# Two edits to a two-layer mixer kernel: weight halves summed by an accumulating transfer, and a gate product in 512-column matmuls

## The chip, the cores and the metric

The kernel runs on one core of one Trainium2 chip. The metric is the device time of one execution in microseconds (us); less is better. The time before is the median of three runs.

## The reference

Two layers act on 256 tokens of width 2048, together with 256 context tokens, all in float32. Layer 0 is a Fourier mixer, layer 1 an attention mixer. The parts that the change touches are the input projection of layer 0 and the gate of layer 1:

```python
def _fourier_branch(h, w_in, w_mix):
    b, n, _ = h.shape
    u, z = jnp.split(h @ w_in, 2, axis=-1)
    ug = u.reshape(b, n, FNET_GROUPS, FNET_GROUP_DIM).astype(jnp.float32)
    f = jnp.fft.fft2(ug, axes=(1, 3), norm='ortho').real.astype(h.dtype)
    f = jnp.einsum('bngc,gcd->bngd', f, w_mix).reshape(b, n, D_BRANCH)
    return f * jax.nn.silu(z)

def _attention_branch(h, hc, w_in, sink, rows, cols, need_ctx):
    ...
    q, k, v, z = jnp.split(h @ w_in, [D_BRANCH, D_BRANCH + kvw, D_BRANCH + 2 * kvw], axis=-1)
    ...                      # banded attention with a sink, 64 heads of 64, 8 key/value heads
    y = jnp.moveaxis(o, 0, 1).reshape(b, n, D_BRANCH) * jax.nn.silu(z)
```

Each layer computes shift, scale and gate from `silu(c) @ ada_w + ada_b`, normalizes its input, runs its branch and adds `gate * (y @ w_out)`. A last normalization follows. There are 16 Fourier groups of 256 channels, and the branch is 4096 wide.

## The kernel before

Every large product is made of three matmuls (`mm3`, L72): each operand is split into a high part (a cast to fp32r on ScalarE, L60) and a low part (the rest, formed on VectorE, L61), and high*high, high*low and low*high are accumulated in PSUM.

The program is written with a tile framework. It gives each engine a queue that runs in order, and a scheduler with a simulated timeline decides the order of the instructions in these queues. So the order on an engine is fixed when the program is built, and an instruction that waits holds up all that stand behind it.

**Projection of layer 0 (`load_uh`, `split_uh`, and the loop over `g`).** The two-dimensional transform is real and symmetric, so channel `j` and channel `256-j` of a group are used as a sum and a difference. The weights are laid out so that one load of 1016 KB (`raw`, a pool of three buffers, issued on SyncE's queue) holds for 8 blocks of 128 rows two halves of 127 channels side by side: `v[:, :, 0, :]` and `v[:, :, 1, :]`. A group has two such loads (`kh` 0 and 1). For each, `load_uh` forms the difference in a tile `wm` (GpSimd, L122) and the sum in place in `raw` (VectorE, L123). `split_uh` then makes four tiles from them (`wml`, `wmh`, `wpl`, `wph`) in a pool of eight, so one group fills the pool, and a half can be split only when TensorE has used the same half of the group before. On TensorE a group runs: `load_m(g)` (10 matmuls, on the mixing weights, `mt` formed by VectorE in L239 and L240), the differences' part (48 matmuls), the mix of the group before (14), the sums' part (48). The results of the mix go to DRAM by two transfers on GpSimd's queue (`fd`, L386).

**The rest of layer 0.** The gate `z` and the output product run after this, with the sums for the adaptive norms on VectorE beside them.

**Layer 1 (`emit_unit`, and the loop that calls it).** The attention loop has 66 steps. A step forms the scores of one half-unit (`stage_s`), the products with the values of an earlier one (`stage_o`), the transposes of the one before (`stage_t`), and two "filler" units between them: an eighth of a query projection, half of a gate block, or a step of the output product. A gate block `("z", b)` is 128 channels of `z`: 16 blocks `k` of the inner dimension, three matmuls of 256 columns each, into the first half of a PSUM bank. `hx1[k]` holds the high part of the input in columns 0 to 255 and the low part in columns 256 to 511. After the last `k`, ScalarE takes tanh (L782) and VectorE completes silu (L783). There are 32 gate blocks.

Of the kernel before, what the change touches and what calls it, by code (L numbers as in the profile page):

```python
# [10 lines left out]
F32 = mybir.dt.float32  # L11
F32R = mybir.dt.float32r
AF = mybir.ActivationFunctionType
ALU = mybir.AluOpType
AX = mybir.AxisListType

P = 128
D = 2048
KT = D // P
DB = 4096  # L20
NB = DB // P
N = 256
# [6 lines left out]
def tile_dit(ctx: ExitStack, tc: tile.TileContext, a: dict, out: bass.AP):  # L29
    nc = tc.nc  # L30
    V, S, PE, GP = nc.vector, nc.scalar, nc.tensor, nc.gpsimd
# [8 lines left out]
    def psum():  # L40
        return pp.tile([P, 512], F32, tag="ps", name="ps")
# [30 lines left out]
    def mm3(o, wh, wl, xh, xl, start, stop):  # L72
        PE.matmul(o, wh, xh, start=start, stop=False)  # L73
        PE.matmul(o, wh, xl, start=False, stop=False)  # L74
        PE.matmul(o, wl, xh, start=False, stop=stop)  # L75
# [43 lines left out]
    def load_uh(g, kh, ld=raw):  # L119
        v = ld(a["wu"][g, kh])[:, : 8 * 2 * 127].rearrange("p (k s c) -> p k s c", k=8, s=2)  # L120
        m = wsp.tile([P, 8, 127], F32, tag="ws", name="wm")
        GP.tensor_tensor(m, v[:, :, 0, :], v[:, :, 1, :], op=ALU.subtract)  # L122
        V.tensor_tensor(v[:, :, 0, :], v[:, :, 0, :], v[:, :, 1, :], op=ALU.add)  # L123
        return v[:, :, 0, :], m

    def split_uh(v, m):
# [8 lines left out]
    def load_u(g):  # L135
        return [split_uh(*f) for f in [load_uh(g, kh) for kh in range(2)]]
# [10 lines left out]
    with tc.tile_pool(name="st", reuse_waits="tile", bufs=1, side="right") as st:  # L147
# [55 lines left out]
        for nb in range(4):  # L203
# [11 lines left out]
            for j in range(4):  # L215
                o = psum()
                for s in range(2):
                    for tt in range(2):
                        q = slice(j * P, (j + 1) * P)
# [90 lines left out]
    for g in range(G):  # L310
        if g == 1:
            w = []
            for kh in range(2):
                f = load_uh(g, kh)
                with tc.issue_after(f0_end):
                    w.append(split_uh(*f))
        else:
            w = load_u(g) if g else w0
# [30 lines left out]
        if g == 0:  # L349
            o = psum()  # L350
            ov = o[0:32, 0:260].rearrange("p (s j) -> p s j", s=2)
            for k in range(KT):
                h, l = hx[k]
                q = slice(k * 32, (k + 1) * 32)
# [75 lines left out]
    with tc.tile_pool(name="yp", reuse_waits="tile", bufs=32) as ypool:  # L430
# [19 lines left out]
        with tc.tile_pool(name="zp", reuse_waits="tile", bufs=2) as zp:  # L450
# [10 lines left out]
            for kg in range(4):  # L461
# [7 lines left out]
                for j in range(4):  # L469
                    k = kg * 4 + j  # L470
                    wh, wl = w[j // 2]
                    for b in range(4):
                        q = slice((j % 2) * 512 + b * P, (j % 2) * 512 + (b + 1) * P)
# [6 lines left out]
            for b in range(4, NB):  # L480
# [3 lines left out]
                o = psum()  # L484
                for k in range(KT):
                    wh, wl = w[k // 8]
                    q = slice((k % 8) * P, (k % 8 + 1) * P)
# [29 lines left out]
        for i in range(32):  # L517
            sw, kg = i // 16, i % 16
            if kg == 0:
                o = [psum() for _ in range(8)]  # L520
# [11 lines left out]
            for j, b in [(j, b) for b in range(8) for j in range(2)] if edge else [(j, b) for j in range(2) for b in range(8)]:  # L532
                q = slice(b * P, (b + 1) * P)
# [16 lines left out]
    o = psum()  # L550
# [8 lines left out]
    o = psum()  # L559
# [27 lines left out]
    with tc.tile_pool(name="h1", reuse_waits="tile", bufs=16) as h1p:  # L587
        hx1 = []
        v2 = [[None] * 2 for _ in range(4)]
        kT = []  # L590
        with tc.tile_pool(name="kvp", reuse_waits="tile", bufs=2) as kvp:
            hc1 = []
            for k in range(KT):
# [3 lines left out]
                for s, h in ((0, hx), (1, hc)):  # L597
                    q = slice(s * N, (s + 1) * N)
# [5 lines left out]
            o = [[psum() for _ in range(2)] for _ in range(4)]  # L604
            for kg in range(8):
                w = ws_split(raw(a["wkv"][kg]))
                for j in range(2):
                    k = kg * 2 + j
                    wh, wl = w[j]
                    for tb in range(4):  # L610
                        h = (hx1, hc1)[tb // 2][k]
                        c = (tb % 2) * P
                        for kv in range(2):
                            q = slice(kv * 512, (kv + 1) * 512)
# [15 lines left out]
            for hp in range(4):  # L630
                o = psum()
# [10 lines left out]
        with tc.tile_pool(name="at", reuse_waits="tile", bufs=2) as at:  # L642
# [19 lines left out]
            def o1_step(k, os_, wh, wl):  # L662
                while len(yh) <= min(k + 2, NB - 1) and (len(yh) < 20 or fin):
                    y_split(len(yh))
                for tb in range(2):
                    mm3(os_[tb], yh[k][:, tb * P : (tb + 1) * P], yh[k][:, N + tb * P : N + (tb + 1) * P], wh, wl, k == 0, k == NB - 1)
# [13 lines left out]
            def finish_q(hk, oq):  # L680
                qr = []
                for tb in range(2):
                    t = act()
                    if hk == 0:
                        roped(t, oq[tb], tb, actp, "act")
                    else:
                        t0 = act()
                        S.copy(t0, oq[tb])
                        roped(t, t0, tb, actp, "act", GP)
                    qr.append(t)  # L690
                prep_kk(hk)
                for p2 in range(2):
                    defer.append((slot[0], lambda p2=p2: q_turn(hk, p2, qr)))
# [38 lines left out]
            def prep(u):  # L732
                kind, n, i, _ = u
                if kind == "o":
                    if i == 1:
                        return None
                    return w1_next()
                src = (kind, n, i // 2)
                if src not in raws1:
                    raws1[src] = raw(a["wq"][n, i // 2] if kind == "q" else a["wz1"][n])  # L740
                return half_split(raws1[src], i % 2)
# [3 lines left out]
            def emit_unit():  # L745
                if pos[0] >= len(ulist):
                    return
                u = ulist[pos[0]]
                if pos[0] not in ready:
                    ready[pos[0]] = prep(u)  # L750
                if pos[0] + 1 < len(ulist):
                    ready[pos[0] + 1] = prep(ulist[pos[0] + 1])
                w = ready.pop(pos[0])
                pos[0] += 1
                kind, n, i, o = u
                if kind == "o":
                    if n == 0 and i == 0:
                        oA.extend([psum(), psum()])
                    if i == 0:
                        curw[0] = w  # L760
                    o1_step(n * 2 + i, oA, *(t[:, i * 512 : (i + 1) * 512] for t in curw[0]))
                    return
                wh, wl = w
                if kind == "q":
                    if i == 0:
                        o += [psum(), psum()]
                    for j in range(2):
                        k = i * 2 + j
                        q = slice(j * 512, (j + 1) * 512)
                        for tb in range(2):  # L770
                            mm3(o[tb], hx1[k][:, tb * P : (tb + 1) * P], hx1[k][:, N + tb * P : N + (tb + 1) * P], wh[:, q], wl[:, q], k == 0, k == KT - 1)
                    if i == 7:
                        finish_q(n, o)
                else:
                    if i == 0:
                        o.append(psum())
                    for k in range(i * 8, i * 8 + 8):
                        q = slice((k % 8) * P, (k % 8 + 1) * P)
                        mm3(o[0][:, 0:N], wh[:, q], wl[:, q], hx1[k][:, 0:N], hx1[k][:, N : 2 * N], k == 0, k == KT - 1)
                    if i == 1:  # L780
                        th = at.tile([P, N], F32, tag="th", name="th", bufs=3)
                        S.activation(th, o[0][:, 0:N], AF.Tanh, scale=0.5)  # L782
                        V.scalar_tensor_tensor(th, th, 1.0, o[0][:, 0:N], op0=ALU.add, op1=ALU.mult)  # L783
                        szs[n] = th
                        emit_y(n)

# [2 lines left out]
            def emit_y(blk):  # L789
                if blk not in szs or (blk, 1) not in obs or blk in ydone:  # L790
                    return
                ydone.add(blk)
                if blk % 2 == 0:
                    y1.append(act())
                V.scalar_tensor_tensor(y1[blk // 2][:, (blk % 2) * N : (blk % 2 + 1) * N], obs[blk, 1], 0.5, szs.pop(blk), op0=ALU.mult, op1=ALU.mult)
# [61 lines left out]
            for i in range(first):  # L857
                emit_unit()
                if i >= 8 and defer:
                    defer.pop(0)[1]()  # L860

            def filler():
                j = slot[0]
                slot[0] += 1
                emit_unit()
                if defer and defer[0][0] + 2 < j:
                    defer.pop(0)[1]()
# [16 lines left out]
        with tc.tile_pool(name="fin", reuse_waits="tile", bufs=1) as fp:  # L884
# [28 lines left out]
            o = [[psum() for _ in range(2)] for _ in range(2)]  # L913
            for kg in range(16):
                w = ws_split(raw(a["wo1b"][kg]))
                for j in range(2):
                    k = kg * 2 + j
                    wh, wl = w[j]
                    for tb in range(2):
                        for c in range(2):  # L920
                            q = slice(c * 512, (c + 1) * 512)
# [4 lines left out]
            o = [psum() for _ in range(2)]  # L926
# [148 lines left out]
```

## Time and profile before

| | us |
|---|---|
| median of three runs | 1885.29 (1885.03 to 1887.53) |
| the profiled execution | 1881.67 |
| its span | 1879.8 |

| engine | busy us | share of the span | instructions |
|---|---|---|---|
| TensorE, matmuls (PE) | 1835.5 | 98% | 10433 |
| TensorE, weight loads (PEld) | 1583.7 | 84% | 10433 |
| VectorE (DVE) | 1396.9 | 74% | 2711 |
| ScalarE (ACT) | 929.7 | 49% | 1602 |
| GpSimd (POOL) | 240.5 | 13% | 206 |

The mean granted clock of TensorE is 0.988. The projection of layer 0 lies between about 100 and 348 us, the attention loop of layer 1 between about 1180 and 1700 us.

How to read the rows: a row of a group of instructions has line, engine, operation, output <- inputs, shapes, count | busy us, mean ns of one | idle time of the engine before them and what ended it. A row of a timeline begins with the start in us from the start of the span and the duration in us. Matmuls overlap, so the duration of one is longer than the distance to the next. A row of waits says which engine waited at which line for what: total us, times, longest us. A row of a DMA queue has packets, MB, and the share of the 16 DMA engines' time; a row of transfers has their count, KB each, and the median us from issue to landing.

### The profile page before, as it was taken

To read this page: it belongs to the slowest core of one execution; us is meant where nothing else is said; L and a number is where in the kernel's file an instruction comes from. 1 tells how busy PE (TensorE), PEld (TensorE's weight loads), DVE (VectorE), ACT (ScalarE), POOL (GpSimd) and SP (SyncE) were. 2 spreads that over 40 slices of the span, in tenths; PEclk is the share of its full clock that TensorE was granted. 3 is DMA by queue.
4 is the path that set the end of the run, shared out by engine and by line. 5 is a ranking of instruction groups with operands and counts; after the bars stand their busy time and mean duration, and the time that the engine had idled before them with its cause. 6 is when DMAs were issued, how large, how long until landed. Compare 5 with 4: busy or idle time off the path is not lost.

```text
span 1879.8 us, 27439 instructions
## 1 busy us (share of the span) xinstructions
PE 1835.5 (98%) x10433; PEld 1583.7 (84%) x10433; DVE 1396.9 (74%) x2711; ACT 929.7 (49%) x1602; POOL 240.5 (13%) x206
## 2 busy tenths in 40 slices
PE   6899999999999999999999999999999999999997
PEld 4479999888888888888888787889989989998886
DVE  4469999787777789687984835788778787787455
ACT  3334444442222233324221524888888888887343
POOL 0034444200000000000000001112221220200001
PEclk8899999999999999999999999999999999999999
DMA  9965555656665546763575323333333333434543
GB/s 365 387 258 201 200 202 189 233 218 232 244 232 214 224 179 256 269 236 134 224 270 222 129 90 135 135 132 115 129 118 135 113 135 126 167 132 169 192 179 135
DMA packets 60533, 359.67 MB, mean 191 GB/s; under 512 B 7601, under 2 KB 7745, under 8 KB 25329
## 3 DMA queue, kind: packets, MB, share of 16 engines
q1 hardware_dynamic: 49104, 324.83, 46.7%
q0 software_dynamic: 6720, 25.34, 3.6%
q10 hardware_dynamic: 4576, 7.74, 1.3%
q8 instruction: 82, 1.34, 0.3%
q14 instruction: 51, 0.41, 0.1%
HBM read 345.30 MB, written 12.59 MB: 190 GB/s over the span
## 4 chain that ended last, share of the span: by engine, by line
PE 88%; DVE 4%; DMA 3%; issue 2%; ACT 1%; POOL 1%; ACTq 0%; POOLq 0%; DVEq 0%; SPq 0%
PE ps L73 25%; PE ps L74 25%; PE ps L75 25%; PE ps L830 3%; PE ps L845 2%; PE ps L844 2%; PE ps L811 1%; PE ps L810 1%; DMA raw<-in_awp 1%; DMA raw<-in_wu 1%; PE ps L180 1%; POOL wm L122 1%; DVE mt L239 1%; DVE wpl L61 1%; DVE wml L61 0%
## 5 line engine op out<-in xcount | busy, mean ns | idle before, releaser
L61 DVE TENSOR_TENSOR wl<-raw,wh 128x1024 fp32r<-128x1024 f32 x333 | 423.7, 1274 | 291.1 <-ACT wh L60 288.8
L60 ACT CAST wh<-raw 128x1024 fp32r<-128x1024 f32 x333 | 349.4, 1051 | 566.2 <-PE ps L74 507.0
L74 PE MATMUL ps<-act,wh 128*128 128x512 f32 x1024 | 398.3, 389 | 0.0
L73 PE MATMUL ps<-act,wh 128*128 128x512 f32 x1024 | 394.1, 389 | 0.0
L75 PE MATMUL ps<-act,wl 128*128 128x512 f32 x1024 | 391.1, 389 | 0.0
L73 PEld LDWEIGHTS ps<-act,wh 128*128 128x128 f32 x1024 | 192.2, 188 | 39.8
L75 PEld LDWEIGHTS ps<-act,wl 128*128 128x128 f32 x1024 | 192.2, 188 | 39.9
L74 PEld LDWEIGHTS ps<-act,wh 128*128 128x128 f32 x1024 | 192.2, 188 | 39.8
L417 DVE CUSTOM_DVE_ANT_0 raw<-raw,cb 128x512 f32<-128x512 f32 x256 | 172.5, 688 | 16.4 <-DMA raw<-in_adw 12.6
L73 PE MATMUL ps<-h,wh 128*128 128x256 f32 x512 | 147.1, 287 | 0.0
L74 PE MATMUL ps<-h,wh 128*128 128x256 f32 x512 | 144.8, 283 | 0.0
L75 PE MATMUL ps<-h,wl 128*128 128x256 f32 x512 | 144.7, 283 | 0.0
L417 DVE CUSTOM_DVE_ANT_0 junk<-raw,cb 128x512 f32<-128x512 f32 x192 | 131.7, 686 | 14.1 <-ACT cb L409 7.1
L74 PE MATMUL ps<-wl,h 128*128 128x512 f32 x320 | 125.5, 392 | 1.4 <-DVE wl L61 1.4
L73 PE MATMUL ps<-wh,h 128*128 128x512 f32 x320 | 124.7, 398 | 0.2 <-ACT h L600 0.2
L75 PE MATMUL ps<-wh,h 128*128 128x512 f32 x320 | 124.9, 392 | 0.0
L122 POOL TENSOR_TENSOR wm<-raw 128x1016 f32<-128x1016 f32 x32 | 87.7, 2740 | 195.8 <-DMA raw<-in_wu 195.3
L812 DVE CUSTOM_DVE_ANT_0 ps<-ps,mask,nsink 128x512 f32<-128x512 f32 x128 | 92.0, 753 | 10.9 <-PE ps L811 10.6
L73 PEld LDWEIGHTS ps<-h,wh 128*128 128x128 f32 x512 | 97.3, 190 | 1.3
L815 ACT ACTIVATE p<-ps,mx 128x512 f32<-128x512 f32 x128 | 87.3, 687 | 21.3 <-DVE mx L812 20.3
L74 PEld LDWEIGHTS ps<-h,wh 128*128 128x128 f32 x512 | 97.4, 190 | 0.0
L75 PEld LDWEIGHTS ps<-h,wl 128*128 128x128 f32 x512 | 97.3, 190 | 0.0
(302 smaller groups left out, 3785.3 us busy)
## 6 DMA issues: line engine op xcount, KB each, us to landing
raw<-in_wz SPq DMA_DIRECT2D x64, 1024.0 KB, 4.8
raw<-in_adw SPq DMA_DIRECT2D x64, 1024.0 KB, 4.8
raw<-in_awp SPq DMA_DIRECT2D x32, 1024.0 KB, 9.5
raw<-in_wo SPq DMA_DIRECT2D x32, 1024.0 KB, 5.5
raw<-in_wq SPq DMA_DIRECT2D x32, 1024.0 KB, 4.8
raw<-in_wu SPq DMA_DIRECT2D x32, 1016.0 KB, 5.4
raw<-in_wo1b SPq DMA_DIRECT2D x16, 1024.0 KB, 4.8
act<-in_xT POOLq DMA_DIRECT2D x32, 256.0 KB, 5.2
```

The costliest lines, as they stand in the source:

```text
L60: S.copy(h, src)
L61: V.tensor_tensor(l, src, h.bitcast(F32), op=ALU.subtract)
L73: PE.matmul(o, wh, xh, start=start, stop=False)
L74: PE.matmul(o, wh, xl, start=False, stop=False)
L75: PE.matmul(o, wl, xh, start=False, stop=stop)
L122: GP.tensor_tensor(m, v[:, :, 0, :], v[:, :, 1, :], op=ALU.subtract)
L417: V.tensor_tensor_reduce(junk if s == 0 and i < 3 else wf, wf, cb[:, s, kq * 512 : kq * 512 + 512], 1.0, 0.0, ALU.mult, ALU.add, acc[:, i, ...
L812: V.tensor_tensor_reduce(o, o, mask[:, tb, :], -0.125, nsink[:, i : i + 1], ALU.add, ALU.min, mx[:, tb : tb + 1])
L815: S.activation(pt[:, tb, :], so[tb], AF.Exp, bias=mx[:, tb : tb + 1], scale=-1.0, accum_out=sm[:, tb : tb + 1])
L830: PE.transpose(o[:, (kt * 2 + tb) * P : (kt * 2 + tb + 1) * P], pt[:, tb, c : c + P], ident)
L844: PE.matmul(oo[:, 0:N], st, ph[:, q], start=kb == 0, stop=False)
L845: PE.matmul(oo[:, 0:N], st, pl[:, q], start=False, stop=kb == 3)
```

## The change

In the projection, the first two groups stay as they were. For groups 2 to 15 the difference is formed on VectorE, and the sum by a transfer from GpSimd's queue that reads the second half once more from HBM and adds it to the first half in `raw`. It may go out only when VectorE has read the first half.

In layer 1 the gate product multiplies `wh` with high and low part at once (512 columns: high product in columns 0 to 255, cross product in 256 to 511) and `wl` with the high part (256 columns, added to the first half). The two halves of the bank are added at the end: ScalarE copies the second half to a tile `zs` (one buffer), VectorE adds the first, and tanh and the completion of silu read `zs`.

```diff
     def load_uh(g, kh, ld=raw):
         v = ld(a["wu"][g, kh])[:, : 8 * 2 * 127].rearrange("p (k s c) -> p k s c", k=8, s=2)
         m = wsp.tile([P, 8, 127], F32, tag="ws", name="wm")
-        GP.tensor_tensor(m, v[:, :, 0, :], v[:, :, 1, :], op=ALU.subtract)
-        V.tensor_tensor(v[:, :, 0, :], v[:, :, 0, :], v[:, :, 1, :], op=ALU.add)
+        if g < 2:
+            GP.tensor_tensor(m, v[:, :, 0, :], v[:, :, 1, :], op=ALU.subtract)
+            V.tensor_tensor(v[:, :, 0, :], v[:, :, 0, :], v[:, :, 1, :], op=ALU.add)
+        else:
+            V.tensor_tensor(m, v[:, :, 0, :], v[:, :, 1, :], op=ALU.subtract)
+            b = a["wu"][g, kh].rearrange("p (k s c) -> p k s c", k=8, s=2)[:, :, 1, :]
+            nc.gpsimd.dma_start(out=v[:, :, 0, :], in_=b, accum_op=ALU.add)
         return v[:, :, 0, :], m
...
                     for k in range(i * 8, i * 8 + 8):
                         q = slice((k % 8) * P, (k % 8 + 1) * P)
-                        mm3(o[0][:, 0:N], wh[:, q], wl[:, q], hx1[k][:, 0:N], hx1[k][:, N : 2 * N], k == 0, k == KT - 1)
+                        for part in (0, 1) if k < KT - 1 else (1, 0):
+                            if part == 0:
+                                PE.matmul(o[0], wh[:, q], hx1[k], start=k == 0, stop=k == KT - 1)
+                            else:
+                                PE.matmul(o[0][:, 0:N], wl[:, q], hx1[k][:, 0:N], start=False, stop=False)
                     if i == 1:
                         th = at.tile([P, N], F32, tag="th", name="th", bufs=3)
-                        S.activation(th, o[0][:, 0:N], AF.Tanh, scale=0.5)
-                        V.scalar_tensor_tensor(th, th, 1.0, o[0][:, 0:N], op0=ALU.add, op1=ALU.mult)
+                        zs = at.tile([P, N], F32, tag="zs", name="zs", bufs=1)
+                        S.copy(zs, o[0][:, N : 2 * N])
+                        V.tensor_tensor(zs, o[0][:, 0:N], zs, op=ALU.add)
+                        S.activation(th, zs, AF.Tanh, scale=0.5)
+                        V.scalar_tensor_tensor(th, th, 1.0, zs, op0=ALU.add, op1=ALU.mult)
```

## The prediction

> **What bounds the kernel now.** I read the page first: the busy shares and the chain that ended last.
>
> ```profile
> span 1879.8 us, 27439 instructions
> ...
> PE 1835.5 (98%) x10433; PEld 1583.7 (84%) x10433; DVE 1396.9 (74%) x2711; ACT 929.7 (49%) x1602; POOL 240.5 (13%) x206
> ...
> PE 88%; DVE 4%; DMA 3%; issue 2%; ACT 1%; POOL 1%; ACTq 0%; POOLq 0%; DVEq 0%; SPq 0%
> ```
>
> TensorE is the bound over the whole run, so an edit pays only where it takes time off TensorE, or removes one of its few gaps; it costs where it opens a gap. Next come the two stretches that the change touches: the middle of the Fourier projection (150 to 350 us) and the attention loop of layer 1 (1200 to 1700 us). Columns: stretch, length, busy time of each engine, granted clock, share of the DMA engines, GB/s.
>
> ```profile
> 150.00:350.00 200.00, 198.26 (x1629) 197.10 (x1628) 184.97 (x241) 91.74 (x181) 87.69 (x64) 1.00 0.61 211
> 1200.00:1700.00 500.00, 500.00 (x3427) 463.08 (x3427) 398.12 (x762) 419.31 (x815) 86.89 (x73) 1.00 0.36 129
> 250.00:300.00 50.00, 50.00 (x417) 50.00 (x416) 48.92 (x56) 22.96 (x44) 22.18 (x13) 1.00 0.57 197
> ```
>
> In the projection TensorE lacks 1.74 us in 200, VectorE is 92% busy, and the DMA engines are busy 57% of the time where the stage runs evenly (250 to 300). In layer 1 TensorE has no gap, and ScalarE is 84% busy. Nearly all of the 1.74 us lies in three places, read from stretches of 2 us:
>
> ```profile
> 178.00:180.00 2.00, 1.57 (x13) 1.36 (x12) 2.00 (x4) 2.00 (x4) 0.00 (x0) 1.00 0.45 147
> 208.00:210.00 2.00, 1.37 (x11) 1.16 (x11) 2.00 (x4) 2.00 (x4) 0.00 (x0) 1.00 0.49 117
> 346.00:348.00 2.00, 1.47 (x12) 1.25 (x11) 1.76 (x6) 1.44 (x4) 1.10 (x3) 1.00 1.01 381
> ```
>
> In the first two VectorE is full (2.00): 0.43 + 0.63 = 1.06 us lost to a late VectorE. The third is the hand-over to the next stage, which the change leaves alone.
>
> The timeline of TensorE gives the rhythm of one group of the projection: the sums' part (wph), load_m (ch), the differences' part (wmh), the mix (pqh), the next sums.
>
> ```profile
> 282.99 0.29 PE L73 MATMUL ps<-act,wph 128*127 128x260 f32 x1
> ...
> 288.90 0.28 PE L73 MATMUL ps<-mh,ch 128*128 128x256 f32 x1
> ...
> 290.08 0.28 PE L73 MATMUL ps<-act,wmh 128*127 128x256 f32 x1
> ...
> 295.80 0.28 PE L73 MATMUL ps<-mh,pqh 127*128 127x256 f32 x1
> ...
> 297.47 0.29 PE L73 MATMUL ps<-act,wph 128*127 128x260 f32 x1
> ```
>
> A group takes 297.47 - 282.99 = 14.48 us, and two weight halves must be loaded, combined and split in it.
>
> **Layer 1: the gate product.** Before, each of 16 k takes three 256-column matmuls; after, one of 512 columns (wh against high and low side by side) and one of 256. What a matmul costs is the distance between starts, not its duration, since they overlap:
>
> ```profile
> 1281.28 0.28 PE L74 MATMUL ps<-h,wh 128*128 128x256 f32 x1
> ...
> 1283.92 0.28 PE L75 MATMUL ps<-h,wl 128*128 128x256 f32 x1
> ```
> ```profile
> 1259.79 0.39 PE L73 MATMUL ps<-wh,h 128*128 128x512 f32 x1
> ...
> 1261.60 0.39 PE L75 MATMUL ps<-wh,h 128*128 128x512 f32 x1
> ```
> ```profile
> 1253.76 0.40 PE L73 MATMUL ps<-wh,h 128*128 128x512 f32 x1
> 1254.00 0.40 PE L74 MATMUL ps<-wl,h 128*128 128x512 f32 x1
> 1254.23 0.28 PE L845 MATMUL ps<-pl,act 128*128 128x256 f32 x1
> 1254.35 0.28 PE L844 MATMUL ps<-ph,act 128*128 128x256 f32 x1
> ```
>
> The first pair spans 22 starts of the gate product: 2.64 / 22 = 0.120 us each, 0.360 per k. The second spans 8 starts of 512 columns: 1.81 / 8 = 0.226. So a k would take 0.226 + 0.120 = 0.346. Where both widths stand mixed (third fence) a 512 takes 0.23 to 0.24 and the 256 behind it 0.12, so 0.35 or 0.36. The saving per k is 0.014 us by the clean rows, 0.010 by the mixed 0.35, nothing by 0.36; times 16 k and 32 blocks, 512 in all: 7.2, 5.1 or 0. I take 6 us: the new sequence alternates, as the mixed rows do, but regularly, so I set it between the first two.
>
> Each of the 32 blocks gains a ScalarE copy and a VectorE add, both 128x256 out of PSUM; tanh and the following multiply now read SBUF. The nearest rows are the two operations there today:
>
> ```profile
> L783 DVE SCALAR_TENSOR_TENSOR th<-th,ps 128x256 f32<-128x256 f32 x32 | 13.2, 412 | 0.0
> L782 ACT ACTIVATE th<-ps 128x256 f32<-128x256 f32 x32 | 12.1, 379 | 0.0
> ```
>
> So 32 x 0.38 = 12 us more on ScalarE: (419 + 12) / 494 = 87% instead of 84%; 32 x 0.41 = 13 us on VectorE: (398 + 13) / 494 = 83%. Neither is the bound, and softmax results are used one loop step after they are made, so I cost this at 0. The cover is that step's slack; if it is gone, what is queued behind the copy on ScalarE are the exponentials and the weight casts, and TensorE waits for both. In the queues as built the tanh does not stand right behind its copy: exponentials and a weight cast lie between, which cover the wait for VectorE's add. The bank is given back after the add, as it was after the multiply. The bound is all of the saving (6 us).
>
> **Projection: VectorE and GpSimd.** For 14 of 16 groups (28 halves) VectorE drops the add and takes the subtraction of the same shape; GpSimd drops the subtraction and issues a transfer.
>
> ```profile
> L122 POOL TENSOR_TENSOR wm<-raw 128x1016 f32<-128x1016 f32 x24 | 66.4, 2768 | 92.6 <-DMA raw<-in_wu 92.6
> L61 DVE TENSOR_TENSOR wpl<-raw,wph 128x1016 fp32r<-128x1016 f32 x26 | 40.2, 1545 | 0.0
> L123 DVE TENSOR_TENSOR raw<-raw 128x1016 f32<-128x1016 f32 x25 | 30.3, 1211 | 8.8 <-POOL wm L122 8.8
> L386 POOL DMA_DIRECT2D fd<-ft x28 | 15.4, 551 | 14.6 <-ACT ft L385 14.1
> L239 DVE TENSOR_TENSOR mt<-m 128x256 f32<-128x256 f32 x12 | 13.7, 1144 | 0.0
> L240 DVE TENSOR_TENSOR mt<-m 128x256 f32<-128x256 f32 x12 | 5.0, 416 | 0.0
> ```
>
> VectorE's own count is even: 1.21 us out, 1.21 in. But L239 and L240 do the same work and take 1144 and 416 ns: L239 runs beside GpSimd's subtraction and waits for it. With that gone VectorE gets back 12 x 0.73 = 9 us from L239 and 26 x (1.545 - 1.211) = 9 us from wpl, and the 1.06 us of gaps go. The Trainium skill, page "SBUF — State Buffer", section "Who interferes with whom", says that a VectorE instruction with two SBUF inputs contends with a GpSimd instruction that reads SBUF; the trace agrees with the two rows above. I book -1 us (bounds 0 and -1.7). What is late next is TensorE itself, which is full.
>
> The new wait on VectorE: the subtraction now waits for the raw load itself, where GpSimd waited before (92.6 us in the row). In the changed program's order the subtraction of half 0 stands just before the evacuation of an earlier group's sums. The raw load is issued when an older buffer's split is done:
>
> ```profile
> SPq L46 <- DVE wpl L61: 172.4, 26, 9.4
> ```
> ```profile
> q0 software_dynamic: 3020, 9.91, 12.9%
> ...
> raw<-in_wu SPq DMA_DIRECT2D x23, 1016.0 KB, 5.4
> fd<-ft POOLq DMA_DIRECT2D x28, 256.0 KB, 3.8
> ...
> act<-in_xT POOLq DMA_DIRECT2D x12, 256.0 KB, 5.4
> ```
>
> The load lands 5.4 us after its issue; three buffers at two per 14.48 us give 21.7 us per turn, so it is there in time. Cost 0, unless loads become late (below).
>
> **The accumulating transfer.** No row shows one. It reads 508 KB again from HBM, reads as much of the destination, and writes it, in runs of 508 bytes. Two questions.
>
> Latency: in the built order, the transfer of half 0 of group g+1 goes out as the sums' part of g-1 ends (288.90 in the rows), and the cast that needs it stands behind the mix, in the sums' part of g; its target buffers come free halfway through that part, at 297.47 + 2.95 = 300.4. That is 12 us without any wait, and some 16 before the casts and splits queued behind it on ScalarE and VectorE make the next differences' part late. A 256 KB transfer of GpSimd lands in 3.8 to 5.4 us. For 508 KB, worst case: 5.4, plus 5.4 for the bytes (next paragraph), plus an issue eight times as long as the 0.55 us row, for eight times as many runs (4.4): 15 us. At best 6. So latency is covered, and GpSimd's queue too: two issues of at most 4.4 and two stores of 0.55 in 14.48 us. The stores queued behind an issue are late by up to 4.4 us, in a group of slack.
>
> Throughput: GpSimd's queue moved 9.91 MB in 12.9% of 200 us, so 2.6 us of all 16 engines per MB, 1.35 us for 0.52 MB. A second read of the same size makes 2.7; short pieces at half that rate make 5.4. Per group the engines have 0.57 x 14.48 = 8.25 us of work now. Two transfers make that 10.95, 13.65 or 19.05 us, against 14.48. I take the middle, since the read of the destination is certain and nothing here shows short pieces to be slow: 94% full, hidden under TensorE, cost 0.
>
> The Trainium skill, page "DMA: Bandwidth & Descriptors", section "Specifications", speaks against this: 512 B is the smallest transfer at line rate, and below it the engine reads, modifies and writes. The runs here have 508. No run here shows it; by that rule the upper case would hold.
>
> **The sum.** -6 (gate) -1 (gaps) = -7 us. From the profiled execution, 1881.7 us (its span 1879.8 and 1.9 around it), that gives 1874.7; the median of the three timed runs stands 3.6 higher, at 1885.3, which gives 1878.
>
> **The rivals.**
> *The DMA engines become the bound* (slower). Place: groups 2 to 15, from the point where one transfer takes more than (14.48 - 8.25) / 2 = 3.1 us of all engines, 2.3 times the plain rate. Then the raw loads come late, the subtraction waits in VectorE's queue with everything behind it, and TensorE starves. Halfway between the two upper cases, 4.05 us each: 16.35 us a group, +1.87 x 14 = +26, less 6 from the gate: 1905. At 5.4 each: 4.57 x 14 = +64, 1943. For it: 94% is near full already, and the runs are short. Against: 2.7 us is below the point. This is the skill's rule with a price.
> *The gate's saving does not come* (no change). Either the 512 takes 0.24 in the alternation, or ScalarE at 87% makes TensorE wait in a loop that had no gap: 0 to 3 us of the 6 left, 1881 to 1884. For it: the mixed rows. Against: the clean rows, and idle time on ScalarE of 16%.
> That the change would not do what it says is excluded: the changed program as built has the 28 transfers on GpSimd's queue and the 512-column matmuls on TensorE's.
>
> **How the numbers follow.** Forecast 0.55, DMA-bound 0.32, saving lost 0.13. The forecast's own range is 1875 (gate 7.2, gaps 1.7, and a little) to 1881. The range reaches from 1874 to 1910, which takes in the DMA rival up to 4.2 us a transfer and leaves out its tail, about 0.15. 0.2%, about what a measurement of this kernel can tell from no change, is 3.8 us: faster 0.55, same 0.13, slower 0.32.
>
> **What would show it.** Right: groups of the projection still 14.5 us apart, DMA share there near 0.9, L239's successor near 0.42 us, no "POOL wm" rows after group 1; in layer 1, 0.346 to 0.35 us per k and no idle row on TensorE. Wrong: a period above 15 us with ScalarE's wph cast waiting for DMA, a landing over 16 us, or an issue on GpSimd of many microseconds; in layer 1, gaps before the transposes of p.

## The result, and the profile after

| | before | after | ratio, 95% interval |
|---|---|---|---|
| median of 20 runs each, us | 1886.82 | 1892.33 | 1.0023 (1.0012 to 1.0034) |
| the same on another chip (17 and 8 runs) | 1886.25 | 1891.08 | 1.0028 (1.0011 to 1.0046) |
| profiled execution, its span | 1879.8 | 1887.1 | |

The change made the kernel slower by some 5 us. The page, as before: span, then busy time by engine.

```profile
span 1887.1 us, 26515 instructions
...
PE 1828.3 (97%) x9921; PEld 1555.3 (82%) x9921; DVE 1375.3 (73%) x2743; ACT 943.5 (50%) x1634; POOL 206.7 (11%) x206
```

TensorE has 7.2 us less to do (1835.5 before) and yet the span is 7.3 us longer: gaps came in. The score matmuls of layer 1 (`kkh`) date them; they carry different lines in the two kernels. First the kernel before, then after: the `qa` row has the first start, the `qb` row the last.

```profile
L810 PE MATMUL ps<-kkh,qa x64: 389/389/477, 1185.9 to 1697.6; 128*128 128x512 f32 x64
L810 PE MATMUL ps<-kkh,qb x64: 388/390/478, 1186.8 to 1704.0; 128*128 128x512 f32 x64
```
```profile
L822 PE MATMUL ps<-kkh,qa x64: 387/389/477, 1196.8 to 1704.6; 128*128 128x512 f32 x64
L822 PE MATMUL ps<-kkh,qb x64: 389/389/478, 1197.7 to 1711.6; 128*128 128x512 f32 x64
```

The loop begins 10.9 us later and takes 514.8 us instead of 518.1: the gate edit gave 3.3, everything ahead of layer 1 lost 10.9. The stretches of the projection show where (columns as in the prediction; the last is the attention loop):

```profile
200.00:250.00 50.00, 50.00 (x419) 50.00 (x418) 39.71 (x59) 25.38 (x45) 13.86 (x13) 1.00 1.10 266
250.00:300.00 50.00, 46.97 (x390) 46.76 (x389) 32.71 (x50) 20.90 (x40) 12.29 (x12) 1.00 1.03 238
300.00:350.00 50.00, 41.77 (x341) 40.93 (x339) 36.28 (x57) 20.38 (x39) 11.44 (x12) 0.99 0.97 245
...
1250.00:1700.00 450.00, 450.00 (x2636) 395.43 (x2634) 370.02 (x717) 387.99 (x766) 79.06 (x67) 1.00 0.38 131
```

From 150 to 250 us TensorE is better served than before (from 200 to 250 it is busy for 50.00 of 50 us, 49.37 before, and VectorE for 39.7 instead of 46.4). After that it starves: 3 us of 50 lost, then 8. Its timeline at the turn, the first matmul of the sums' part of two groups and the first of two load_m parts:

```profile
264.89 0.29 PE L73 MATMUL ps<-act,wph 128*127 128x260 f32 x1
279.34 0.29 PE L73 MATMUL ps<-act,wph 128*127 128x260 f32 x1
288.44 0.39 PE L73 MATMUL ps<-mh,ch 128*128 128x256 f32 x1 [3.03 <-ACT mh L60]
...
305.44 0.39 PE L73 MATMUL ps<-mh,ch 128*128 128x256 f32 x1 [2.31 <-ACT mh L60]
```

Groups came 14.45 us apart (279.34 - 264.89), and then 17.0 (305.44 - 288.44), with TensorE waiting for ScalarE's cast `mh`. That cast hardly waits for anything of its own (not at all the first time, 0.46 us for `mt` the second): it stands in ScalarE's queue behind weight casts, and the first of these, a `wph`, waits for its transfer. The queue view for 150 to 350 us (packets, MB, share; then the transfers with the median landing) and the groups of instructions there:

```profile
q0 software_dynamic: 28177, 20.09, 63.3%
q1 hardware_dynamic: 3820, 27.56, 37.0%
...
raw<-in_wu SPq DMA_DIRECT2D x23, 1016.0 KB, 6.6
raw<-in_wu POOLq DMA_DIRECT2D x24, 508.0 KB, 9.0
fd<-ft POOLq DMA_DIRECT2D x26, 256.0 KB, 4.7
```
```profile
L128 POOL DMA_DIRECT2D raw<-in_wu x24 | 35.3, 1471 | 60.6 <-DVE wm L126 54.5 <-DVE apl L61 4.4 <-issue 1.0
L61 DVE TENSOR_TENSOR wpl<-raw,wph 128x1016 fp32r<-128x1016 f32 x25 | 30.4, 1215 | 30.1 <-ACT wph L60 29.8
L126 DVE TENSOR_TENSOR wm<-raw 128x1016 f32<-128x1016 f32 x24 | 29.0, 1209 | 0.0
L244 DVE TENSOR_TENSOR mt<-m 128x256 f32<-128x256 f32 x12 | 5.0, 417 | 0.0
```

Three readings. The subtraction on VectorE (L126) never waits, so raw loads are in time. VectorE's split waits for the cast behind the transfer (29.8 us). And the transfer is dear, measured by the time of its packets: the stores and one input load on that queue, 7.1 MB at the 2.6 us per MB of the kernel before, are 9.2% of the time, which leaves (63.3 - 9.2)% of 200 us over 24 transfers, 4.5 us of all 16 DMA engines each, where I had 2.7. Both a dear transfer and a late one are thus there; which of them costs had to be tried.

### The profile page after: what moved, and what is told of

It reads as the page before. It is cut to its first block, busy times and chain, and to the rows that moved or that the text cites. A ratio compares the mean times of both kernels' runs of the same rounds, so it can differ in the third digit from the quotient of the medians.

```text
span 1887.1 us, 26515 instructions
## 1 busy us (share of the span) xinstructions
PE 1828.3 (97%) x9921; PEld 1555.3 (82%) x9921; DVE 1375.3 (73%) x2743; ACT 943.5 (50%) x1634; POOL 206.7 (11%) x206
## 4 chain that ended last, share of the span: by engine, by line
PE 78%; DVE 2%; ACT 1%; issue 1%; DMA 1%; POOL 0%; ACTq 0%; POOLq 0%; DVEq 0%
PE ps L73 20%; PE ps L74 20%; PE ps L75 20%; PE ps L786 6%; PE ps L788 3%; PE ps L842 3%; PE ps L857 2%; PE ps L856 2%; PE ps L822 1%; PE ps L823 1%; DMA raw<-in_wu 1%; ACT wh L60 0%; PE ps L705 0%; DVE wl L61 0%; DVE act L510 0%
## 5 line engine op out<-in xcount | busy, mean ns | idle before, releaser
L73 PEld LDWEIGHTS ps<-act,wh 128*128 128x128 f32 x1024 | 192.2, 188 | 39.7
L786 PE MATMUL ps<-h,wh 128*128 128x512 f32 x512 | 187.0, 400 | 0.0
L788 PE MATMUL ps<-h,wl 128*128 128x256 f32 x512 | 138.1, 280 | 0.0
L786 PEld LDWEIGHTS ps<-h,wh 128*128 128x128 f32 x512 | 96.1, 188 | 19.0
L824 DVE CUSTOM_DVE_ANT_0 ps<-ps,mask,nsink 128x512 f32<-128x512 f32 x128 | 92.1, 753 | 12.2 <-PE ps L823 11.3
L61 DVE TENSOR_TENSOR pl<-ps,ph 128x512 fp32r<-128x512 f32 x128 | 83.7, 685 | 10.0 <-ACT ph L60 9.0
L832 ACT ACTIVATE p<-p,sm 128x512 f32<-128x512 f32 x128 | 85.4, 717 | 7.8 <-DVE sm L830 7.8
L74 PE MATMUL ps<-wl,ys 128*128 128x512 f32 x212 | 83.3, 393 | 0.0
```

Of the source, the lines that this page charges most:

```text
L61: V.tensor_tensor(l, src, h.bitcast(F32), op=ALU.subtract)
L786: PE.matmul(o[0], wh[:, q], hx1[k], start=k == 0, stop=k == KT - 1)
L788: PE.matmul(o[0][:, 0:N], wl[:, q], hx1[k][:, 0:N], start=False, stop=False)
L824: V.tensor_tensor_reduce(o, o, mask[:, tb, :], -0.125, nsink[:, i : i + 1], ALU.add, ALU.min, mx[:, tb : tb + 1])
L832: S.activation(pt[:, tb, :], pt[:, tb, :], AF.Copy, scale=sm[:, tb : tb + 1])
```

## The experiments

Each time stands against runs of the kernel before on the same chip. "The change" is the whole edit.

**Each half alone.**

```diff
 e1_gate_only: load_uh as before; gate product as in the change
 e2_proj_only: load_uh as in the change; gate product as before
```

> The gate edit alone; the projection as before. In the trace of the changed kernel eight steps of the attention loop take 67.04 us instead of 67.62, so both theories (transfers too many for the DMA engines; waits behind the transfer) expect 8 x 0.58 = 4.6 us less, less up to 1.3 us where the loop starts: 3.3 to 4.6 us, ratio 0.9975 to 0.9982. If the gate edit gains nothing and the change's projection costs less than I think, the ratio is 1.000.

> The projection edit alone; the gate as before. If the two edits add up, this is slower by the 11.0 us by which the projection ended later in the changed kernel's trace, ratio 1.005 to 1.006, with the gaps of TensorE after 280 us, a DMA share above 1.0, and 17 us a group. If the gate edit were the loss, 1.000.

Gate alone: 1882.85 against 1883.72, ratio 0.9999 (0.9986 to 1.0011). Projection alone: 1894.87, ratio 1.0061 (1.0045 to 1.0078). So the projection edit is what costs. In the trace of the first the loop takes 514.8 us, in that of the second 518.1, as above; but the first shows no gain in the whole time. Up to layer 1 it has the instructions of the kernel before in the same order on every engine, and yet its loop began at 1193.2 instead of 1185.9 us: the old projection, with VectorE over 90% busy, varies by several us from run to run (its twelve runs went from 1875.98 to 1889.72). The interval leaves no room for a gain of 3.3 us in the whole time (that would be 0.9982), so in these runs something outside the loop cost about as much, and no run shows what. A later pair of runs, with and without the gate edit, does show the gain (0.9954 and 0.9972, 3.4 us apart).

**Half of the transfers, and longer pieces.** Theory A: the DMA engines' throughput is the bound (8.25 us of other work a group and two transfers of 4.5 us make 17.25, near the 17.0 seen). If so, halving the transfers, or making them cheaper, cures it.

```diff
 e3_half
-        if g < 2:
+        if g < 2 or kh == 0:
 e4_runs4k: the two halves of a row lie one after the other in HBM and in raw
-            nc.gpsimd.dma_start(out=v[:, :, 0, :], in_=b, accum_op=ALU.add)
+            nc.gpsimd.dma_start(out=r[:, : 8 * 127], in_=a["wu"][g, kh, :, 8 * 127 :], accum_op=ALU.add)
```

> Both edits, but the accumulating transfer for half 1 of each group only; half 0 as before (GpSimd and VectorE). Theory of throughput: one transfer at 4.5 us of all engines makes 8.25 + 4.5 = 12.75 us of DMA work in a 14.48 us group, so no gaps, the projection ends at 346 to 348 us, and the gate's gain is left: 4 to 6 us less than before, ratio 0.997 to 0.998. Rival (the latency of the single transfer, and the casts queued behind it): the transfer for half 1 still lands after 9 us, about half of the 11 us stays, and the ratio is 1.000 or above.

> Both edits, with the weights laid out so that each half is one run of 4064 bytes a partition instead of eight of 508; same bytes, same additions. If the short runs make the transfer cost 4.5 us of the engines instead of 2.7, then 8.25 + 5.4 = 13.65 us a group: no gaps, 5 to 6 us less than before, ratio 0.997. If the addition itself is the price (4.5 us whatever the run length), about 17 us a group in the second half of the stage, and the ratio stays near 1.002.

Both stayed slow: 1890.73, ratio 1.0040 (1.0026 to 1.0053), and 1898.85, ratio 1.0083 (1.0070 to 1.0096). With longer pieces the transfers did become cheaper, 3.3 us each by the same working (6.3 MB of stores), and landed in 7.9 us. Queue view and waits of that kernel, 150 to 350 us:

```profile
q0 software_dynamic: 5463, 19.07, 47.7%
...
raw<-in_wu POOLq DMA_DIRECT2D x24, 508.0 KB, 7.9
```
```profile
DVE wm L127 <- DMA raw<-in_wu: 53.9, 12, 5.6
...
PE ps L75 <- DVE wml L61: 12.6, 10, 2.3
```

The stretch from 150 to 350 us in the two runs, first half of the transfers, then longer pieces:

```profile
150.00:350.00 200.00, 189.78 (x1549) 187.13 (x1548) 168.25 (x224) 89.89 (x172) 63.86 (x51) 1.00 0.79 220
```
```profile
150.00:350.00 200.00, 185.92 (x1503) 183.17 (x1501) 140.42 (x211) 85.40 (x160) 34.86 (x48) 0.99 0.86 246
```

The share of the DMA engines was 0.79 and 0.86, and TensorE still lost 10 to 14 us of 200. Theory A cannot say why. The run with half of the transfers came out on its rival's side: the transfers that were left still landed late, in 10.2 us (median), on less loaded engines; but nearly all of the loss stayed, not half. In the run with longer pieces the scheduler put the subtraction in VectorE's queue where its raw load had not landed (53.9 us, none in the change), and the splits behind it came late. So these two runs have another order of the queues as well, and neither isolates the transfer.

**A fourth buffer.** Theory B: latency. A raw buffer is now kept through the landing of the transfer as well, and three buffers do not give the time. The room for a fourth comes from single buffers for load_m's two split tiles and from moving a staging tile; a control has these but no fourth buffer.

```diff
 e6_raw4 (e7_raw4_4k: the same with the longer pieces; e9_gate_raw4: the same with the old projection)
+    def raw_up(src):
+        t = up.tile([P, 2032], F32, tag="rawx", name="rawx", bufs=1)
+        nc.sync.dma_start(t, src)
+        return t
-        return [split_uh(*f) for f in [load_uh(g, kh) for kh in range(2)]]
+        return [split_uh(*f) for f in [load_uh(g, kh, raw_up if g % 2 and kh else raw) for kh in range(2)]]
 e6_raw4, e7_raw4_4k, e9_gate_raw4 and the control e10_singles
-            lr = ua.tile([P, 2, GD], F32R, tag="ml", name="ml")
+            lr = ua.tile([P, 2, GD], F32R, tag="ml", name="ml", bufs=1)
...
 e8_dummy (old projection with the gate edit)
+            nc.gpsimd.dma_start(out=dum[0], in_=b, accum_op=ALU.add)
```

> The changed kernel once more, for its spread and as the measure of the three runs beside it. In the first profile its projection groups ran 14.4 us for ten groups and then 17.0, 17.0, 16.8 us; layer 1 began 10.9 us later than in the kernel before. The gate product of layer 1 should take 514.8 us again between the first and the last score matmul (518.1 before). Both theories expect 1888 to 1893 us.

> The change with a fourth buffer for the raw weight halves (every fourth half of groups 2 to 15 goes to a buffer of its own; its room comes from single buffers for load_m's two split tiles). Theory A, the DMA engines' throughput: two transfers of 4.5 us beside 8.25 us of other work are 17.25 us a group whatever the number of buffers, so the late groups stay at 17 us, and the time stays 1888 to 1893. Theory B, the turn of the buffers: load 8, subtraction 1.2, issue 1.5, transfer 9, cast and split 2.3 make 22 us, against 3/2 x 14.48 = 21.7 us that three buffers give; four give 29 us. Then every group takes 14.5 us, TensorE has no gap after group 3, and the time is 1879 to 1884.

> The same fourth buffer, and the host layout with runs of 4064 bytes, in which a transfer cost the engines 3.3 us. Theory A: 8.25 + 6.6 = 14.85 us a group, where three buffers took 16.2: 1880 to 1885. Theory B: 14.5 us a group, 1879 to 1884. If it stays at 16 us a group (1895 to 1900), neither holds, and what holds VectorE up in this layout is something else, such as the order of its queue.

> The gate edit and the old projection path (difference on GpSimd, sum on VectorE), with seven eighths of each accumulating transfer added, to a tile that nobody reads; so the load on the DMA engines without the longer turn of the raw buffers. Theory A: 8.25 + 2 x 3.9 = 16.1 us a group once the slack is used, so at least 8 us lost: 1890 or more. Theory B: nobody waits for the transfers, groups stay near 14.5 us, and the time is within 3 us of the gate edit alone (1882.9); a raw load that lands later by the shared engines costs at most a few us.

> The gate edit and the old projection path, with the fourth raw buffer and the single split tiles of the four-buffer run, so that run without the transfer and without moving the difference. If the fourth buffer by itself is what made 1880 us, this gives 1880 too (ratio 0.997). If the buffer only pays for the transfer's longer stay, this stands where the gate edit alone stood: 1882 to 1884 (ratio 0.998 to 1.000), with TensorE short of work by 1 to 4 us between 150 and 350 us because VectorE is over 90% busy there.

> The whole change with load_m's split tiles single and the constants' staging tile moved, but with three raw buffers: the four-buffer run without its fourth buffer. Turn of the buffers: as slow as the change, 1888 to 1893, with groups of 17 us late in the stage. If this comes to 1880, it was the reordering by the single tiles, not the buffer, that made the four-buffer run fast.

| | median us | ratio, 95% interval |
|---|---|---|
| the change again | 1891.08 | 1.0028 (1.0011 to 1.0046) |
| the change with four buffers | 1879.99 | 0.9972 (0.9962 to 0.9981) |
| its control, three buffers | 1894.92 | 1.0048 (1.0032 to 1.0064) |
| longer pieces, four buffers | 1900.88 | 1.0086 (1.0071 to 1.0101) |
| gate edit, old projection, four buffers | 1901.50 | 1.0091 (1.0075 to 1.0107) |
| gate edit, old projection, transfers to an unread tile | 1921.03 | 1.0196 (1.0181 to 1.0211) |

The fourth buffer turns the change into a gain. The window of that run, and its queues there:

```profile
150.00:350.00 200.00, 200.00 (x1660) 200.00 (x1658) 156.57 (x231) 95.28 (x179) 56.24 (x60) 1.00 1.09 265
```
```profile
q0 software_dynamic: 29372, 21.20, 66.3%
q1 hardware_dynamic: 4032, 28.39, 37.0%
```

TensorE is busy for all of the 200 us with more such transfers in them (26 instead of 24) and a higher DMA share than in the change (1.09, 1.06 there). The transfers cost 4.2 us each there by the same working. So the DMA engines' throughput is not what bounds the change, and theory A falls. The control excludes the single tiles, and the fourth buffer by itself is no gain either: with the old projection TensorE lost 19 us of the 200, which neither theory had expected, and with the longer pieces it lost 10. The row of the old projection with four buffers:

```profile
150.00:350.00 200.00, 181.17 (x1464) 177.56 (x1465) 165.30 (x210) 83.85 (x161) 72.98 (x48) 1.00 0.50 172
```

The run with the unread tile was to be the counter-test and did not become one: each transfer adds to the tile that the last one wrote, and so waits for it on GpSimd (95.8 us), with the subtractions of the old path queued behind.

```profile
POOL dum L126 <- DMA dum<-in_wu: 95.8, 24, 6.7
```

**The addition alone.** The fourth buffer also changed the order of the queues. This run does not: every engine has the instructions of the change in the same order, and only the addition is left out, so that the second half replaces the sum.

```diff
 e5_plain
-            nc.gpsimd.dma_start(out=v[:, :, 0, :], in_=b, accum_op=ALU.add)
+            nc.gpsimd.dma_start(out=v[:, :, 0, :], in_=b)
```

> The change with the transfer's addition left out: the same 508 KB in the same 508-byte runs are written over the first half instead of added to it (so the sum is replaced by the second half). Every engine's queue has the same instructions in the same order as in the change, so a difference comes from the transfer alone. Turn of the buffers: a plain transfer should land in 5 to 7 us where the accumulating one took 9 to 11, and cost the engines 1.4 to 3 us; the turn falls from 23.5 to below 21.7 us, and the time to 1880 to 1884. If the order of the queues that comes with the transfer is what costs, this is as slow as the change, 1889 to 1893.

1871.96 us, ratio 0.9937 (0.9922 to 0.9952): some 16 us less than the change by the ratios, and 8 less than theory B had expected at best. The queue view:

```profile
q0 software_dynamic: 6307, 21.91, 34.0%
...
raw<-in_wu POOLq DMA_DIRECT2D x24, 508.0 KB, 6.0
```

Without the addition the transfer lands in 6.0 us instead of 9.0, and costs 1.7 us of the engines (after 10.2 MB of stores and input loads). Its packets are also fewer, 6307 on the queue instead of 28177 (under 512 bytes, over all queues, 1976 instead of 27074): the pieces of 508 bytes travel one by one only where they are added. GpSimd issues it in 0.90 us instead of 1.47. The edit takes away all of this at once, so the 16 us are the price of the accumulating transfer as a whole. The order of the queues is the same in both runs, so no part of the difference comes from a change of order.

**Why three more us of landing cost so much** is in the change's own trace: GpSimd's issues of transfers, each second one; then, for 262 to 300 us, what lies between two of them.

```profile
222.63 1.46 POOL L128 DMA_DIRECT2D raw<-in_wu  x1 [6.81 <-DVE wm L126]
...
237.74 1.47 POOL L128 DMA_DIRECT2D raw<-in_wu  x1 [0.47 <-DVE wm L126]
...
252.91 1.49 POOL L128 DMA_DIRECT2D raw<-in_wu  x1 [0.26 <-DVE wm L126]
...
269.21 1.49 POOL L128 DMA_DIRECT2D raw<-in_wu  x1 [0.38 <-issue]
...
285.99 1.44 POOL L128 DMA_DIRECT2D raw<-in_wu  x1 [0.28 <-DVE wm L126]
```
```profile
280.03 1.04 ACT L60 CAST wph<-raw 128x1016 fp32r<-128x1016 f32 x1 [3.71 <-issue]
```
```profile
281.11 1.22 DVE L61 TENSOR_TENSOR wpl<-raw,wph 128x1016 fp32r<-128x1016 f32 x1 [3.92 <-ACT wph L60]
...
284.49 1.21 DVE L126 TENSOR_TENSOR wm<-raw 128x1016 f32<-128x1016 f32 x1
```

How long the transfers issued at 237.74 and at 269.21 took to land:

```profile
raw<-in_wu POOLq DMA_DIRECT2D x1, 508.0 KB, 6.8
```
```profile
raw<-in_wu POOLq DMA_DIRECT2D x1, 508.0 KB, 10.8
```

It is a ring. A transfer goes out at 269.21 and lands 10.8 us later; its cast starts at 280.03, 10.82 after the issue; the split follows at 281.11; and behind that split, in VectorE's queue, stands the subtraction for the half after the next, at 284.49 to 285.70, which releases the next transfer but one at 285.99. That subtraction could have run earlier: its raw load went out at about 270.6, when an older split ended, and landed 8.2 us later, at about 279. Round the ring: 10.82 + 1.08 + 4.59 + 0.29 = 16.78 us. All of it but the transfer is 5.96, so a ring of 14.48 leaves a transfer 8.5 us.

From 222.63 on these transfers go out 15.1, 15.2, 16.3 and 16.8 us apart, while TensorE still needs a group every 14.5. The first two steps are not the ring's: the transfers of 222.63 and 237.74 landed in 6.7 and 6.8 us, and VectorE reached the subtraction late because operations on TensorE's results stand ahead of it. Those of 252.91, 269.21 and 285.99 landed in 9.5, 10.8 and 10.5 us, and from there on the ring is too long. The difference eats the cover, and when that is gone, at 288 us, TensorE falls into the ring's step. The second profile of the change repeats it: 15.1, 15.2, 16.4 and 17.0 us apart, with landings of 6.9, 6.7, 9.6 and 11.0.

In the run without the addition the same transfers go out 14.7, 15.3, 15.7 and 15.6 us apart and land in 5.6, 5.5, 7.7 and 9.6 us (median of all 6.0, within the 8.5); then the step falls to 13.4, and TensorE loses 1.4 us of the 200 instead of 11.3. So theory B holds in its core (latency, not throughput), but not as I had stated it: not the turn of the buffers closes the ring, but the order in VectorE's queue. Why the landing grows within the stage is not shown, and another order with the same transfers and three buffers was not tried.

With four buffers the order of VectorE's queue is another one. GpSimd and ScalarE of that run, one half:

```profile
239.40 1.47 POOL L128 DMA_DIRECT2D rawx<-in_wu  x1 [2.32 <-DVE wm L126]
```
```profile
252.44 1.06 ACT L60 CAST wph<-rawx 128x1016 fp32r<-128x1016 f32 x1
```

That is 13.0 us from issue to cast, and the cast waits for nothing. The landings themselves are no shorter there (medians 8.0 us and, into the fourth buffer, 11.5).

**Without transfer and without GpSimd.** Theory C: what the change gains it gains by taking GpSimd off VectorE's side, so both operations might as well go to VectorE.

```diff
 e11_dve (with the gate edit), e12_dve_raw4 (with four buffers too), e14_dve_only (without the gate edit); against the kernel before
-        GP.tensor_tensor(m, v[:, :, 0, :], v[:, :, 1, :], op=ALU.subtract)
+        (GP if g < 2 else V).tensor_tensor(m, v[:, :, 0, :], v[:, :, 1, :], op=ALU.subtract)
         V.tensor_tensor(v[:, :, 0, :], v[:, :, 0, :], v[:, :, 1, :], op=ALU.add)
```

> The gate edit, and from group 2 on both the sum and the difference on VectorE: no transfer, nothing on GpSimd but the stores. VectorE has 39.5 us of 50 in the change, and two more operations of 1.21 us a group make 8.4 more: 96%, without the slowing by GpSimd. If the gain of the four-buffer run comes from taking GpSimd off VectorE's back, this is near it, 1880 to 1883; if it comes from the work that VectorE no longer has, this has the gaps of the kernel before or more: 1882 to 1890.

> The same as the run with both operations on VectorE, with the fourth raw buffer. VectorE is what is short there, not buffers, so no difference from that run by more than 2 us.

> Sum and difference of groups 2 to 15 both on VectorE, without the gate edit. With the gate edit the pair took 0.9954 of the kernel before (8.2 us less), and the gate's loop was 3.3 us shorter. If the two add, this is 4 to 6 us faster than before: ratio 0.997 to 0.998, with 518.1 us between first and last score matmul.

1876.35 us, ratio 0.9954 (0.9941 to 0.9968); with four buffers 1878.21, ratio 0.9966 (0.9954 to 0.9979); without the gate edit 1879.27, ratio 0.9972 (0.9959 to 0.9984). The first is better than either case expected of it, and of the kernels that form the sum it is the fastest; the fourth buffer adds nothing, as expected, and the last lies in its expected range. Loops of 514.8 us with the gate edit and 518.1 without show its 3.3 us again. The window of the first, and then a group of the kernel before that shows where VectorE's time comes from, beside the same group here:

```profile
150.00:350.00 200.00, 199.91 (x1651) 199.22 (x1650) 181.76 (x261) 92.58 (x180) 21.43 (x40) 1.00 0.58 208
```
```profile
L61 DVE TENSOR_TENSOR ml<-mt,mh 128x512 fp32r<-128x512 f32 x13 | 20.0, 1537 | 0.0
```
```profile
L61 DVE TENSOR_TENSOR ml<-mt,mh 128x512 fp32r<-128x512 f32 x13 | 8.9, 684 | 0.0
L122 DVE TENSOR_TENSOR wm<-raw 128x1016 f32<-128x1016 f32 x24 | 29.1, 1211 | 0.2
```

VectorE took on 24 subtractions, 29.1 us, and is busy 181.76 us instead of 184.97. TensorE lacks 0.09 us of 200 instead of 1.74.

## Why the prediction was wrong, step by step

- **What bounds the kernel**: right. TensorE has no slack, and the loss came as gaps in the projection. The measured time lies inside the stated range, but that is its width: no mechanism of the prediction gives 1892 us.
- **Gate, 6 us**: the mechanism was right and the size was off; it gave 3.3. The new alternation, in the timeline of the change:

```profile
1435.04 0.40 PE L786 MATMUL ps<-h,wh 128*128 128x512 f32 x1
...
1436.81 0.40 PE L786 MATMUL ps<-h,wh 128*128 128x512 f32 x1
```

  Five k in 1.77 us, 0.354 per k, where I had set 6 us' worth, 0.348. The mixed rows (0.35 to 0.36) were the right ones to go by, and a regular alternation is no better than an irregular one: 512 x (0.360 - 0.354) = 3.1.
- **ScalarE's copy and VectorE's add, cost 0**: right. TensorE is busy 450.00 of 450 us in the loop.
- **Contention relief**: right and undervalued. `mt` took 417 ns and `wpl` 1215, as forecast from 1144 and 1545. I booked 1 us; with both operations on VectorE the projection alone gave 0.28% of the whole, some 5 us, which fits that the old projection loses more in another run than the 1.74 us of the one profile: 3.3 us of the same 200 in the run of the gate edit alone.
- **The subtraction's wait for the raw load, cost 0**: right for the change (0.0 idle). It became real in the runs with longer pieces, under another order of the queue.
- **The transfer's latency, "covered"**: this is the step that failed. Estimate (6 to 15 us) and measurement (6.7 to 14.4, median 9.0) agree; the cover was wrong. I held 12 us, and 16 before TensorE waits, against the transfer of half 0, as a single one that goes out on time. For half 0 it held: issued at 273.71, landed in 9.1 us, cast at 284.75. The transfer of half 1 I did not cost at all, and the ring runs through it: the cast at 280.03 must be half 1's, since TensorE has been on the sums of half 0 since 279.34 and reaches those of half 1 at 282.30. The split for them ends at 282.33. And none of these transfers goes out on time by itself: each stands behind a subtraction that stands behind the split of an earlier one. A cover helps once; a ring has to close in 14.48 us, and it takes 16.8.
- **The transfer's throughput, 2.7 us**: mis-sized, 4.5 measured, above the break-even of 3.1 that I had named. But the break-even itself was no bound: the run with four buffers had such transfers at a share of 1.09 without a gap. A share above 1 also says that time in packets cannot be read as engine time used up. By the rival's own sum 4.5 us a transfer gives 17.25 us a group, 2.77 x 14 - 6 = 33 us more, 1918; the kernel took 1892. My slower rival thus had the right sign and place for the wrong reason, and its subtraction that waits for late raw loads did not occur.
- **The Trainium skill's rule** ("DMA: Bandwidth & Descriptors", "Specifications": transfers below 512 B lose line rate to read-modify-write): the trace agrees in direction. An accumulating transfer costs 4.5 us in pieces of 508 bytes and 3.3 in pieces of 4064, and the upper case of 5.4 was not reached; that the cause is a read-modify-write no run here shows. The longer pieces did not make the kernel faster, so this price alone did not decide.

In the run with longer pieces another ring shows, through the raw load:

```profile
258.51 1.21 DVE L61 TENSOR_TENSOR wpl<-raw,wph 128x1016 fp32r<-128x1016 f32 x1
...
268.36 1.22 DVE L127 TENSOR_TENSOR wm<-raw 128x1016 f32<-128x1016 f32 x1 [4.21 <-DMA raw<-in_wu]
...
274.19 1.21 DVE L61 TENSOR_TENSOR wpl<-raw,wph 128x1016 fp32r<-128x1016 f32 x1
```

The split ends at 259.72 and frees its buffer; the load into it goes out then and lands 8.6 us later; the subtraction has waited for it and starts at 268.36; behind it stands the split that ends at 275.40, 15.68 us after the first. With four buffers the subtractions still waited 25.8 and 26.1 us for raw loads. Open stays why four buffers make the old projection slower (1901.50), and in all these runs that the order of the queues is the cause was not tried by itself.

## What to carry to other kernels

When a transfer is put between two steps that follow each other group after group, do not set its landing against the slack of one passage: go round the ring, from its issue over its consumer and over what stands behind that consumer in an in-order queue to the next issue, and ask whether the sum fits the period. A ring that is too long by 2 us hides for as long as the cover lasts, so look at whether issues drift against the bound engine. And before work is moved from a busy engine to a transfer, see whether that engine is slowed by a neighbour: here it was enough to give it the neighbour's work.

## What the runs showed of the hardware

- An accumulating transfer of 508 KB in pieces of 508 bytes took 4.5 us of packet time on the 16 DMA engines, landed in 9.0 us and took GpSimd 1.47 us to issue; the same bytes written plainly took 1.7 us, landed in 6.0, took 0.90 us to issue, and went out in far fewer packets (6307 on the queue instead of 28177). I had assumed that the addition costs only one more read.
- Next to GpSimd's subtraction, a VectorE operation of 684 ns (`ml`) lasted 1537 ns in the mean, and 684 with that subtraction moved to VectorE, so that VectorE with 29 us more work of its own was 3 us less busy.
- The DMA queues' shares added up to more than 1 (1.09) with TensorE busy for 200.00 of 200 us. It was not free for the loads: raw loads landed in 7.3 us there, 5.4 in the kernel before.
